# One kernel, two decoder layers: two heads' scores with one zero-padded key tile, and matmuls of different column tiles issued in turn

## The chip, the cores and the metric

The kernel runs on one core of a Trainium2 chip. The metric is the device time of one execution, in microseconds (us), lower is better. The core has a matmul engine (TensorE, "PE" in profile rows, with its weight loads as "PEld"), three element-wise engines (VectorE "DVE", ScalarE "ACT", GpSimd "POOL") and a queue that issues transfers (SyncE, "SP"). Each engine works through its own instructions in order and waits for others by semaphores.

## The reference, cut to what matters

Two layers are computed for a prompt of 512 tokens and for 8 samples of 4 tokens each (32 sample tokens). Layer 0 has 8 attention heads of width 64 beside a convolution branch; layer 1 is a gated linear recurrence. The change touches the attention of layer 0 alone. For the prompt it is causal attention over all 512 positions (two blocks of 256, both always chosen):

```python
s_own = jnp.einsum('bhqd,bhkd->bhqk', qc, k_own).astype(jnp.float32) * scale
...
p = jax.nn.softmax(s, axis=-1)
...
return (jnp.einsum('bhqnk,bhqnkd->bhqd', p_sel, v_sel)
        + jnp.einsum('bhqk,bhkd->bhqd', p_own, v_own))
```

For each sample the queries meet 256 cached positions (two pages of 128, found by a page table) and the sample's own 4 new positions.

## The kernel before, in words

All activations lie transposed, features on the 128 partitions and tokens along the free axis. A projection is a sum of `unit` calls (L136 to L145): one unit is 24 matmuls of 128x128 weights with 272 columns, on a high and a low part of weights and inputs (L142, L143, L144). Weight tiles arrive by `wtile`, which also splits them on ScalarE (`wh`, L133) and VectorE (`wl`, L134).

The attention of the prompt works on one pair of heads at a time, `c` = 0 to 3. The 64 features of the pair's first head lie on partitions 0 to 63, those of the second on 64 to 127. `prep(c)` projects q, k, v and the gate, normalises them and transposes the keys into `kT` (L430, one ScalarE copy of 128x512). `attend(...)` then goes over four query blocks `i` of 128 rows. For each head `hh` it computes the scores (L465, 64 rows of contraction, 128, 256, 384 or 512 columns), adds a causal mask with a bfloat16 matmul (L467), takes the maximum (L473, VectorE), the exponential (L476, ScalarE), divides (L478), transposes 128x128 pieces of the probabilities through TensorE (L102), copies them back (`PT`, L483, ScalarE) and multiplies with the values (L485, an output of 64 partitions at `tile_position` 0 or 64). The score tiles `s` have two PSUM banks, the transposes `t` two, the output `o` one.

A matmul of 32-bit operands is two matmul instructions on the engine, each with its weight load; the 64 score products are 32 in the code, the 160 value products 80 and the 128 key products of the samples 64. Transposes are one each.

The samples' stage (L569 to L611) loads each sample's two cached key pages (`kn`, 256 KB each, 8 buffers, by SP) and multiplies them with block-diagonal queries `qbd`: 4 chunks `c` for each page (L576, an output of 32 partitions at `tile_position` 32*n4), for samples n4 = 0 to 3 of a group `g`, with both pages `j` of one sample before the next sample. The new keys follow (L582), then a softmax over 288 columns, then the value pages (`kn` again, L611). The 8 `kn` buffers are shared with squares, sums and the conv gate of layer 0, so pages wait for buffers.

A scheduler decides the order on every engine from the code's order and priorities; `attend` runs at a raised priority, and `unit` work of other stages is put between its steps. Beside all this VectorE does the convolution, 120 multiply-adds of 128x512 (L508). The functions that the diff touches:

Of the kernel before, what the change touches and what calls it, by code (L numbers as in the profile page):

```python
# [9 lines left out]
F32 = mybir.dt.float32  # L10
# [3 lines left out]
AF = mybir.ActivationFunctionType  # L14
# [5 lines left out]
TP = 512  # L20
# [46 lines left out]
def hybrid_step(ctx, tc, xt_in, cache_kt, cache_v, conv_in, hgrn_in, page_table, par_in, k_norm_0,  # L67
# [3 lines left out]
    V, A, G, PE, SP = nc.vector, nc.scalar, nc.gpsimd, nc.tensor, nc.sync  # L71
# [7 lines left out]
    def nm(s):  # L79
        cnt[0] += 1  # L80
        return f"{s}{cnt[0]}"

    def mk(pool, tag, shape, bufs, dt=F32):
        return pool.tile(shape, dt, name=nm(tag), tag=tag, bufs=bufs)

    def bank(tag, cols=512, dt=F32):
        return pp.tile([128, cols], dt, name=nm(tag), tag=tag, bufs={"g": 3, "s": 2, "t": 2, "o": 1}[tag])
# [13 lines left out]
    def transpose(out, in_, np_):  # L101
        PE.transpose(out, in_, ident[:np_, :np_])  # L102

    def split(hi, lo, src, eng=None):
        A.activation(hi, src, AF.Copy)
        (eng or V).tensor_tensor(lo, src, hi, op=ALU.subtract)
# [44 lines left out]
    gq8 = cp.tile([128, 1], F32, name="gq8")  # L151
# [22 lines left out]
    def mtile(key, dt=F32R):  # L174
        m_[key] = mk(hp, "m", [128, T], 2 * KT, dt)
        return m_[key]

    with tc.tile_pool(name="l0", bufs=1) as lp:
# [138 lines left out]
        qbd = lp.tile([128, 4, NS, 32], F32, name="qbd")  # L317
# [51 lines left out]
            uconv(c)  # L369

        aes = ExitStack()

        def prep(c):
            col = c * 128
# [8 lines left out]
            pk = bank("t")  # L383
# [11 lines left out]
            qT = mk(lp, "qT", [128, T], 2)  # L395
# [16 lines left out]
            for hh in range(2):  # L412
                r = slice(64 * hh, 64 * hh + 64)
# [1 line left out]
                V.scalar_tensor_tensor(qbd[r, c, :, o:o + 4], qT[r, TP:T].rearrange("p (n t) -> p n t", t=4),  # L415
                                       gq8[r], rq[r, 8:40].rearrange("p (n t) -> p n t", t=4),
                                       op0=ALU.mult, op1=ALU.mult)
            kT = mk(lp, "kT", [128, TP], 2)
            for i0, i1, n in ((0, 4, 128), (4, 5, TS)):
                k3 = kt[:n, i0:i1].rearrange("p i (h d) -> p (i h) d", d=64)  # L420
                nb = 2 * (i1 - i0)
# [4 lines left out]
            pk = bank("t")  # L426
            pks = bank("t")
            for i, n, sl in TOK:
                transpose(pk[:, sl] if i < 4 else pks[:, :n], kt[:n, i], n)
            A.activation(kT, pk, AF.Copy, scale=gq8[:, 0:1])  # L430
            V.tensor_copy(ksT[:, c], pks[:, :TS])

            w = wtile(w_in_0, 1024 + col)
# [4 lines left out]
            pk = bank("t")  # L438
# [19 lines left out]
        def attend(c, rq, qT, kT, vt, ga):  # L458
            po = bank("o")
            for i in range(4):  # L460
                L = 128 * (i + 1)
                ss = [bank("s"), bank("s")]
                for hh in range(2):
                    r = slice(64 * hh, 64 * hh + 64)
                    PE.matmul(ss[hh][:, :L], qT[r, i * 128:(i + 1) * 128], kT[r, 0:L], start=True, stop=False)  # L465
                for hh in range(2):
                    PE.matmul(ss[hh][:, L - 128:L], identb, causb, start=False, stop=True)  # L467
                for hh in range(2):
                    r = slice(64 * hh, 64 * hh + 64)
                    rqc = rq[:, 2 * i + hh:2 * i + hh + 1]  # L470
                    s = ss[hh]
                    mx = mk(lp, "mx", [128, 4], 4)
                    V.tensor_reduce(mx[:, 0:1], s[:, :L], axis=AX.X, op=ALU.max, negate=True)  # L473
                    A.activation(mx[:, 1:2], mx[:, 0:1], AF.Copy, scale=rqc)
                    P = mk(qp, "PP", [128, 512], 3)
                    A.activation(P[:, :L], s[:, :L], AF.Exp, bias=mx[:, 1:2], scale=rqc, accum_out=mx[:, 2:3])  # L476
                    V.reciprocal(mx[:, 3:4], mx[:, 2:3])
                    V.tensor_scalar_mul(P[:, :L], P[:, :L], mx[:, 3:4])  # L478
                    pT = bank("t")
                    for j in range(i + 1):  # L480
                        transpose(pT[:, j * 128:(j + 1) * 128], P[:, j * 128:(j + 1) * 128], 128)
                    PT = mk(qp, "PT", [128, 512], 3)
                    A.activation(PT[:, :L], pT[:, :L], AF.Copy)  # L483
                    for j in range(i + 1):
                        PE.matmul(po[r, i * 128:(i + 1) * 128], vt[:, j, r],  # L485
                                  PT[:, j * 128:(j + 1) * 128], start=(j == 0), stop=(j == i),
                                  tile_position=(0, 64 * hh))
            mh, ml = mtile(("h", c)), mtile(("l", c))
            V.scalar_tensor_tensor(ga[:, :TP], po, 0.5, ga[:, :TP], op0=ALU.mult, op1=ALU.mult)
            split(mh[:, :TP], ml[:, :TP], ga[:, :TP])  # L490
# [9 lines left out]
        qp = aes.enter_context(tc.tile_pool(name="qk", bufs=1))  # L500

        p0 = prep(0)
        p1 = prep(1)
        with tc.high_priority(offset=300):
            attend(*p0)
        for c in (0, 1, 2, 3):
            for j in range(1, 31):
                V.scalar_tensor_tensor(cy[c][:, :TP], up[c][:, j:j + TP], cw[:, c, j:j + 1], cy[c][:, :TP],  # L508
                                       op0=ALU.mult, op1=ALU.add)

        p2 = prep(2)
        with tc.high_priority(offset=300):
            attend(*p1)
# [24 lines left out]
        with tc.high_priority(offset=300):  # L538
            attend(*p2)
# [25 lines left out]
        ss_, PTs = [], []  # L565
        for g in range(2):
            s = bank("s", 288)
            ss_.append(s)
            for n4 in range(4):  # L569
                n = 4 * g + n4  # L570
                for j in range(2):
                    knT = mk(lp, "kn", [128, T], 8)[:, :512]
                    rg = SP.value_load(pt[0:1, 2 * n + j:2 * n + j + 1], min_val=0, max_val=cache_kt.shape[0] - 1)
                    SP.dma_start(knT, cache_kt[bass.ds(rg, 1)].rearrange("a p c t -> (a p) (c t)"))
                    for c in range(4):
                        PE.matmul(s[32 * n4:32 * n4 + 32, j * 128:(j + 1) * 128], qbd[:, c, n, :],  # L576
                                  knT[:, c * 128:(c + 1) * 128], start=(c == 0), stop=(c == 3),
                                  tile_position=(0, 32 * n4))
            PE.matmul(s[:, 256:288], identb, smb[:, 32 * g:32 * g + 32], start=True, stop=False)
            for n4 in range(4):  # L580
                for c in range(4):
                    PE.matmul(s[32 * n4:32 * n4 + 32, 256:288], qbd[:, c, 4 * g + n4, :], ksT[:, c, :],  # L582
                              start=False, stop=(c == 3), tile_position=(0, 32 * n4))
        for g in range(2):
            s = ss_[g]
# [10 lines left out]
            PT = mk(qp, "PT", [128, 512], 3)  # L596
# [4 lines left out]
        for g in range(2):  # L601
            PT = PTs[g]
            ov = bank("s")
            PE.matmul(ov, PT[:32, 256:384], vsn, start=True, stop=False)
            for j in range(2):
                for n4 in range(4):
                    n = 4 * g + n4
# [4 lines left out]
                              start=False, stop=(j == 1), tile_position=(0, 32 * n4))  # L612
# [406 lines left out]
```

## Time and profile before

| | us |
|---|---|
| three runs | 694.25, 694.40, 694.69 (median 694.4) |
| the profiled execution | 693.45 |
| its span in the trace | 691.7 |
| TensorE busy | 671.8 |
| VectorE busy | 542.6 |
| ScalarE busy | 314.5 |
| GpSimd busy | 70.3 |
| mean granted TensorE clock | 0.99 |

The span runs from the first to the last instruction that the profiler recorded; the profiled execution's own time has 1.75 us around it. "Busy" is the time in which at least one instruction of the engine was running; matmuls overlap in a pipeline, so a TensorE that is busy all the time can still do less per microsecond than it could.

### The profile page before, as it was taken

How to read it: one execution, taken by the hardware profiler on the slowest of the kernel's cores; microseconds unless marked ns; L12 is line 12 of the kernel's file. 1: busy time of each engine (PE TensorE's matmuls, PEld its weight loads, DVE VectorE, ACT ScalarE, POOL GpSimd, SP SyncE). 2: the span in 40 equal slices, each digit the busy share in tenths (PEclk: the TensorE clock that was granted, in tenths of full speed). 3: DMA queues.
4: the chain of work that ended last, by engine and by line, in shares of the span. 5: the costliest groups of instructions: out<-in, count | busy, mean ns of one | idle time of the engine just before them, and what ended most of it. 6: DMA issues, size and time to landing. Idle time of an engine off the chain costs nothing.

```text
span 691.7 us, 14812 instructions
## 1 busy us (share of the span) xinstructions
PE 671.8 (97%) x5806; PEld 598.3 (86%) x5806; DVE 542.6 (78%) x1326; ACT 314.5 (45%) x758; POOL 70.3 (10%) x89
## 2 busy tenths in 40 slices
PE   8899999989999999999998999999999999999997
PEld 7799999867877976857998999989998989899997
DVE  7999999898957975344796987878697878777676
ACT  7332444525556956232665453525253525234221
POOL 5000200000302100000001200102020202020100
PEclk9999999989999999999999999999999999999999
DMA  9412152221111150674454213141313131322213
GB/s 268 155 62 92 65 167 79 77 77 32 56 69 30 63 170 1 176 234 132 159 177 150 65 62 125 64 127 62 127 62 128 62 127 62 111 63 68 76 52 142
DMA packets 34583, 70.51 MB, mean 102 GB/s; under 512 B 7378, under 2 KB 16210, under 8 KB 34514
## 3 DMA queue, kind: packets, MB, share of 16 engines
q1 hardware_dynamic: 34514, 69.58, 31.3%
q8 instruction: 45, 0.74, 0.4%
q14 instruction: 24, 0.20, 0.1%
HBM read 59.84 MB, written 9.73 MB: 101 GB/s over the span
## 4 chain that ended last, share of the span: by engine, by line
PE 91%; DVE 5%; ACT 1%; issue 1%; DMA 1%; SPq 1%; DVEq 0%
PE g L142 22%; PE g L144 22%; PE g L143 22%; PE t L102 5%; PE s L465 3%; PE o L485 3%; PE s L576 2%; PE s L611 2%; PE s L768 1%; PE t L874 1%; PE o L887 1%; PE o L889 1%; DVE wl L134 1%; PE t L907 1%; DMA wr<-in_w_in_dram 1%
## 5 line engine op out<-in xcount | busy, mean ns | idle before, releaser
L142 PE MATMUL g<-h,wh 128*128 128x272 f32 x944 | 277.8, 295 | 7.1 <-ACT f L702 2.6
L143 PE MATMUL g<-h,wh 128*128 128x272 f32 x944 | 276.1, 293 | 2.1 <-DVE h L273 2.1
L144 PE MATMUL g<-h,wl 128*128 128x272 f32 x944 | 276.5, 293 | 0.0
L142 PEld LDWEIGHTS g<-h,wh 128*128 128x128 f32 x944 | 179.7, 191 | 11.5 <-ACT f L702 3.1
L143 PEld LDWEIGHTS g<-h,wh 128*128 128x128 f32 x944 | 179.7, 191 | 4.0 <-DVE h L273 2.8
L144 PEld LDWEIGHTS g<-h,wl 128*128 128x128 f32 x944 | 179.7, 191 | 2.0 <-issue 1.3
L133 ACT ACTIVATE wh<-wr 128x1024 fp32r<-128x1024 f32 (+4 forms) x90 | 88.2, 982 | 109.4 <-PE g L143 101.9
L134 DVE TENSOR_TENSOR wl<-wr,wh 128x1024 fp32r<-128x1024 f32 (+4 forms) x90 | 101.1, 1125 | 22.8 <-ACT wh L133 22.6
L508 DVE SCALAR_TENSOR_TENSOR m<-m,vecs,m 128x512 f32<-128x512 f32 x120 | 84.1, 734 | 0.0
L143 PE MATMUL g<-m,wh 128*128 128x272 f32 x256 | 74.4, 293 | 0.0
L144 PE MATMUL g<-m,wl 128*128 128x272 f32 x256 | 73.5, 290 | 0.0
L142 PE MATMUL g<-m,wh 128*128 128x272 f32 x256 | 73.1, 295 | 0.0
L143 PEld LDWEIGHTS g<-m,wh 128*128 128x128 f32 x256 | 48.2, 188 | 4.3 <-issue 3.1
L142 PEld LDWEIGHTS g<-m,wh 128*128 128x128 f32 x256 | 47.1, 188 | 4.5 <-issue 2.1
L144 PEld LDWEIGHTS g<-m,wl 128*128 128x128 f32 x256 | 48.1, 188 | 1.2 <-DVE tb L642 0.8
L473 DVE TENSOR_REDUCE mx<-s 128x1 f32<-128x128 f32 (+3 forms) x32 | 15.4, 485 | 13.3 <-PE s L467 13.1
L483 ACT ACTIVATE PT<-t 128x128 f32<-128x128 f32 (+3 forms) x32 | 13.9, 434 | 26.0 <-PE t L102 25.7
L485 PE MATMUL o<-PT,vt 128*64 128x128 f32 x160 | 23.9, 283 | 1.6 <-ACT PT L483 1.5
L465 PE MATMUL s<-kT,qT 64*128 64x128 f32 (+3 forms) x64 | 25.2, 482 | 0.0
L910 DVE SCALAR_TENSOR_TENSOR S<-S,tot,t 128x128 f32<-128x128 f32 x64 | 17.7, 342 | 6.3 <-PE t L907 6.2
L485 PEld LDWEIGHTS o<-PT,vt 128*64 128x64 f32 x160 | 16.4, 136 | 6.0 <-ACT PT L483 2.5
L852 DVE TENSOR_TENSOR kk<-kk,tot 128x256 f32<-128x256 f32 (+1 forms) x48 | 20.0, 417 | 0.0
(289 smaller groups left out, 998.6 us busy)
## 6 DMA issues: line engine op xcount, KB each, us to landing
wr<-in_w_in_dram SPq DMA_DIRECT2D x58, 512.0 KB, 3.6
wr<-in_w_out_dram SPq DMA_DIRECT2D x16, 512.0 KB, 3.6
kn<-in_cache_kt_dram SPq DMA_DIRECT2D x16, 256.0 KB, 2.9
kn<-in_cache_v_dram SPq DMA_DIRECT2D x16, 256.0 KB, 3.3
S<-in_hgrn_dram SPq DMA_DIRECT2D x8, 512.0 KB, 3.7
out_hgrns_dram<-S SPq DMA_DIRECT2D x8, 512.0 KB, 2.6
xTall<-in_xt_dram SPq DMA_DIRECT2D x8, 272.0 KB, 4.9
out_y_dram<-xTall SPq DMA_DIRECT2D x8, 272.0 KB, 2.4
```

The lines of the kernel that those rows point to most:

```text
L102: PE.transpose(out, in_, ident[:np_, :np_])
L133: A.activation(wh, raw, AF.Copy)
L134: V.tensor_tensor(wl, raw, wh, op=ALU.subtract)
L142: PE.matmul(ps, wh[:, k - k0, :], ah, start=(k == k0), stop=False)
L143: PE.matmul(ps, wh[:, k - k0, :], al, start=False, stop=False)
L144: PE.matmul(ps, wl[:, k - k0, :], ah, start=False, stop=(k == k1 - 1))
L465: PE.matmul(ss[hh][:, :L], qT[r, i * 128:(i + 1) * 128], kT[r, 0:L], start=True, stop=False)
L473: V.tensor_reduce(mx[:, 0:1], s[:, :L], axis=AX.X, op=ALU.max, negate=True)
L485: PE.matmul(po[r, i * 128:(i + 1) * 128], vt[:, j, r], PT[:, j * 128:(j + 1) * 128], start=(j == 0), stop=(j == i), tile_position=(0, 64 * ...
L508: V.scalar_tensor_tensor(cy[c][:, :TP], up[c][:, j:j + TP], cw[:, c, j:j + 1], cy[c][:, :TP], op0=ALU.mult, op1=ALU.add)
L852: V.tensor_tensor(k3[:, :, 0, :], k3[:, :, 0, :], t3[:, :, 1:2].to_broadcast([128, nblk, hsz]), op=ALU.mult)
L910: V.scalar_tensor_tensor(S0[:, n, :], S0[:, n, :], tots[:, n:n + 1], pn[:, n4 * 128:(n4 + 1) * 128], op0=ALU.mult, op1=ALU.add)
```

## The change

The keys of a pair go into a tile `kz` of 128 x 2 x 512, which has zeros where the other head's features would be; GpSimd clears it once, and ScalarE fills it with two copies of 64x512 in place of one of 128x512. A score product then contracts over all 128 partitions with the same 128x128 weight `qT` for both heads. The value products of a block are written after both heads' softmax, alternating between the heads. The samples' key products take the four samples of a group in turn for each chunk, all with their first pages and then all with their second pages, and so do the products with the new keys.

```diff
+        kz = [lp.tile([128, 2, TP], F32, name=f"kz{b}") for b in range(2)]
+        for b in range(2):
+            for hh in range(2):
+                G.memset(kz[b][64 - 64 * hh:128 - 64 * hh, hh], 0.0)
...
-            kT = mk(lp, "kT", [128, TP], 2)
+            kT = kz[c % 2]
...
-            A.activation(kT, pk, AF.Copy, scale=gq8[:, 0:1])
+            for hh in range(2):
+                r = slice(64 * hh, 64 * hh + 64)
+                A.activation(kT[r, hh], pk[r], AF.Copy, scale=gq8[r, 0:1])
...
                 for hh in range(2):
-                    r = slice(64 * hh, 64 * hh + 64)
-                    PE.matmul(ss[hh][:, :L], qT[r, i * 128:(i + 1) * 128], kT[r, 0:L], start=True, stop=False)
+                    PE.matmul(ss[hh][:, :L], qT[:, i * 128:(i + 1) * 128], kT[:, hh, 0:L], start=True, stop=False)
...
-                    for j in range(i + 1):
+                    PTs.append(PT)
+                for j in range(i + 1):
+                    for hh in range(2):
+                        r = slice(64 * hh, 64 * hh + 64)
                         PE.matmul(po[r, i * 128:(i + 1) * 128], vt[:, j, r],
-                                  PT[:, j * 128:(j + 1) * 128], start=(j == 0), stop=(j == i),
+                                  PTs[hh][:, j * 128:(j + 1) * 128], start=(j == 0), stop=(j == i),
                                   tile_position=(0, 64 * hh))
...
-            for n4 in range(4):
-                n = 4 * g + n4
-                for j in range(2):
+            for j in range(2):
+                kns = []
+                for n4 in range(4):
+                    n = 4 * g + n4
                     knT = mk(lp, "kn", [128, T], 8)[:, :512]
...
-                    for c in range(4):
-                        PE.matmul(s[32 * n4:32 * n4 + 32, j * 128:(j + 1) * 128], qbd[:, c, n, :],
-                                  knT[:, c * 128:(c + 1) * 128], start=(c == 0), stop=(c == 3),
+                    kns.append(knT)
+                for c in range(4):
+                    for n4 in range(4):
+                        PE.matmul(s[32 * n4:32 * n4 + 32, j * 128:(j + 1) * 128], qbd[:, c, 4 * g + n4, :],
+                                  kns[n4][:, c * 128:(c + 1) * 128], start=(c == 0), stop=(c == 3),
                                   tile_position=(0, 32 * n4))
...
-            for n4 in range(4):
-                for c in range(4):
+            for c in range(4):
+                for n4 in range(4):
                     PE.matmul(s[32 * n4:32 * n4 + 32, 256:288], qbd[:, c, 4 * g + n4, :], ksT[:, c, :],
```

The scheduler keeps the order on VectorE the same up to the end of the first pair's attention, and on SP throughout. On TensorE it moves what the code moves. Two places show it; a row gives line, operation, output and inputs by name, the output's shape and a count.

On TensorE, in the attention of the third pair (query blocks 1 and 2, `PT` are the transposed probabilities of one head each), before:

```order
L102 MATMUL t_2506<-cst,PP_2502 128x128 x2
L485 MATMUL o_2448<-PT_2495,vt_1861 64x128 x2
L102 MATMUL t_2526<-cst,PP_2522 128x128 x3
L465 MATMUL s_2552<-kT_1786,qT_1714 128x512
L467 LDWEIGHTS identb
L467 MATMUL s_2552<-causb,identb 128x128
L485 MATMUL o_2448<-PT_2509,vt_1861 64x128 x2
L102 MATMUL t_2542<-cst,PP_2538 128x128 x3
```

and with the change:

```order
L102 MATMUL t_2510<-cst,PP_2506 128x128 x2
L493 MATMUL o_2454<-PT_2501,vt_1867 64x128
L102 MATMUL t_2532<-cst,PP_2528 128x128 x3
L470 MATMUL s_2558<-kz_735,qT_1720 128x512
L472 LDWEIGHTS identb
L472 MATMUL s_2558<-causb,identb 128x128
L493 MATMUL o_2454<-PT_2513,vt_1867 64x128
L493 MATMUL o_2454<-PT_2501,vt_1867 64x128
L493 MATMUL o_2454<-PT_2513,vt_1867 64x128
L102 MATMUL t_2545<-cst,PP_2541 128x128 x3
```

The two value products of one head stood together, a step apart from those of the other head. Now the first product of the first head stands alone where its `PT` is ready, and the other products of both heads follow together, after the second head's `PT`.

On TensorE, where the samples' key products begin, between the last value products of the fourth pair (`kn` with a number is one page), before:

```order
L576 MATMUL s_3080<-kn_3081,qbd 32x128 x4
L576 MATMUL s_3080<-kn_3096,qbd 32x128 x4
L576 MATMUL s_3080<-kn_3111,qbd 32x128 x4
L576 MATMUL s_3080<-kn_3126,qbd 32x128
L485 MATMUL o_2598<-PT_2696,vt_2370 64x128 x3
L102 MATMUL t_2714<-cst,PP_2710 128x128 x4
L576 MATMUL s_3080<-kn_3126,qbd 32x128 x3
L576 MATMUL s_3080<-kn_3141,qbd 32x128 x4
L102 MATMUL t_2732<-cst,PP_2728 128x128 x4
L576 MATMUL s_3080<-kn_3156,qbd 32x128 x4
```

and with the change, from the last chunk of the first group of four pages:

```order
L587 MATMUL s_3086<-kn_3109,qbd 32x128
L587 MATMUL s_3086<-kn_3120,qbd 32x128
L587 MATMUL s_3086<-kn_3147,qbd 32x128
L493 MATMUL o_2604<-PT_2699,vt_2376 64x128
L493 MATMUL o_2604<-PT_2686,vt_2376 64x128
L493 MATMUL o_2604<-PT_2699,vt_2376 64x128
L493 MATMUL o_2604<-PT_2686,vt_2376 64x128
L493 MATMUL o_2604<-PT_2699,vt_2376 64x128
L102 MATMUL t_2720<-cst,PP_2716 128x128 x4
L102 MATMUL t_2734<-cst,PP_2730 128x128 x4
L587 MATMUL s_3086<-kn_3158,qbd 32x128
L493 MATMUL o_2604<-PT_2725,vt_2376 64x128
```

One page's four products stood together, page after page. Now the first four pages' 16 products stand together, chunk by chunk (the last two are the first two rows), followed by one product of the fifth page (`kn_3147`), and the first product of the sixth (`kn_3158`) comes after 5 value products and 8 transposes. A page's buffer is free again only when the last chunk of its group is done.

## Rows read from the trace of the kernel before

**Rows 1.** The page: the chain that ended last, its shares by engine.

```profile
PE 91%; DVE 5%; ACT 1%; issue 1%; DMA 1%; SPq 1%; DVEq 0%
```

**Rows 2.** By stage: start:end, length, busy PE, PEld, DVE, ACT, POOL, clock, DMA share, GB/s.

```profile
100.00:165.00 65.00, 61.59 (x424) 53.89 (x424) 60.35 (x114) 28.06 (x61) 0.66 (x1) 0.95 0.25 75
...
250.00:285.00 35.00, 34.68 (x220) 22.58 (x221) 15.12 (x44) 18.91 (x54) 0.00 (x0) 1.00 0.29 89
285.00:325.00 40.00, 40.00 (x289) 25.42 (x287) 19.67 (x42) 14.00 (x32) 0.00 (x0) 1.00 0.55 178
```

**Rows 3.** Timeline of TensorE around 170 us (start, length, instructions, idle before).

```profile
168.67 1.09 PE L485 MATMUL o<-PT,vt 128*64 128x128 f32 x8 [0.69 <-ACT PT L483]
169.69 0.70 PE L465 MATMUL s<-kT,qT 64*128 64x256 f32 x2
...
170.38 0.60 PE L102 MATMUL t<-cst,PP 128*128 128x128 f32 x4
170.82 0.60 PE L102 MATMUL t<-cst,kr 128*128 128x128 f32 x4
```

**Rows 4.** The same view around 271 us, scores of 512 columns.

```profile
270.45 1.12 PE L465 MATMUL s<-kT,qT 64*128 64x512 f32 x2
271.51 0.23 PE L467 MATMUL s<-causb,identb 128*128 128x128 bf16 x1
271.57 0.50 PE L102 MATMUL t<-cst,PP 128*128 128x128 f32 x3
272.00 1.12 PE L465 MATMUL s<-kT,qT 64*128 64x512 f32 x2
```

**Rows 5.** The chain of waits (start, length, what): scores of 128 columns, first pair.

```profile
107.11 0.42 PE s L465 x4
...
164.39 0.42 PE s L465 x2
```

**Rows 6.** The chain of waits, samples' stage.

```profile
284.92 0.99 PE s L576 x8
...
299.14 0.83 PE s L582 x32
```

**Rows 7.** The chain of waits, layer 1: products on four column tiles in turn.

```profile
418.94 0.57 PE t L897 x16
```

**Rows 8.** Timeline of TensorE, value pages of the samples.

```profile
300.95 1.06 PE L611 MATMUL s<-kn,PT 128*32 128x512 f32 x6
302.51 1.05 PE L611 MATMUL s<-kn,PT 128*32 128x512 f32 x2
```

**Rows 9.** Timeline of TensorE in layer 1: one product alone on one column tile.

```profile
454.47 0.41 PE L901 MATMUL s<-c,cst 128*32 128x128 f32 x2
454.81 0.73 PE L907 MATMUL t<-ve,kts 128*128 128x512 f32 x2
```

**Rows 10.** The chain of waits around 135 us.

```profile
132.70 2.51 DVE m L508 x4
...
137.15 2.65 DVE m L508 x4
```

**Rows 11.** The stage behind that wait, columns as in rows 2.

```profile
140.00:147.00 7.00, 6.51 (x28) 5.99 (x29) 7.00 (x12) 1.55 (x5) 0.00 (x0) 0.52 0.15 45
```

**Rows 12.** Timeline of SP: issues of key pages (start, from first issue to last).

```profile
246.69 1.55 SPq L574 DMA_DIRECT2D kn<-in_cache_kt_dram  x3
...
276.17 0.35 SPq L574 DMA_DIRECT2D kn<-in_cache_kt_dram  x1
```

**Rows 13.** The tile `kn`: time of its transfers.

```profile
DMA to landing us min/median/max: 2.5/2.9/5.4
```

**Rows 14.** The line of the `kT` copy (duration in ns, min/median/max).

```profile
L430 ACT ACTIVATE kT<-t,gq x4: 667/678/688, 103.1 to 247.7; 128x512 f32<-128x512 f32 x4
```

**Rows 15.** Timeline of GpSimd at the start.

```profile
0.88 0.95 POOL L318 MEMSET qbd<- 128x1024 f32 x1
...
4.12 1.09 POOL L186 TENSOR_TENSOR kn<-xTall 128x544 f32<-128x544 f32 x1 [2.29 <-DMA xTall<-in_xt_dram]
```

More of the change, by code (lines that the diff above doesn't have):

```diff
@@ L463, in attend @@
                 for hh in range(2):
-                    r = slice(64 * hh, 64 * hh + 64)
-                    PE.matmul(ss[hh][:, :L], qT[r, i * 128:(i + 1) * 128], kT[r, 0:L], start=True, stop=False)
+                    PE.matmul(ss[hh][:, :L], qT[:, i * 128:(i + 1) * 128], kT[:, hh, 0:L], start=True, stop=False)
                 for hh in range(2):
                     PE.matmul(ss[hh][:, L - 128:L], identb, causb, start=False, stop=True)
+                PTs = []
                 for hh in range(2):
-                    r = slice(64 * hh, 64 * hh + 64)
                     rqc = rq[:, 2 * i + hh:2 * i + hh + 1]
```

## The prediction, made before the changed kernel was run

> **What bounds the kernel now.** I read the chain of waits first, since it says what the end waited for: TensorE holds 91% of it [rows 1]. Then the stages: all that differs lies between 100 and 325 us, and in the last 75 of these TensorE is busy almost without a gap while VectorE and ScalarE are busy for half the time or less [rows 2]. Before 165 us it is otherwise: VectorE works 60.35 of 65 us. So a microsecond taken off TensorE is worth a microsecond in the later stages, less in the first. The question is how much of TensorE's busy time is work; the timeline, read from the start of one group to the start of the next, answers that.
>
> **Scores.** Two instructions of 128 columns (one product) take 0.42 us, two of 512 columns 1.06 us until the mask begins [rows 5, 4]. The difference, 0.64 us for twice 384 columns, is 0.107 us per 128 columns, so 0.21 us of each block of scores doesn't depend on its size. Another 0.10 lies ahead of it: three transposes before the second block take 0.43 us [rows 4], where four before other transposes take 0.44 [rows 3], 0.11 each. I read this 0.31 us as the price of a change from the full array to a tile of it, with the weight load uncovered, and back. With zero padding the scores use the full array, as transposes, masks and projections do. The built program has 31 blocks of scores before (9.6 us of such price) and 32 after, of which 9 follow value products and still pay 0.20 (1.8); the other 23 pay nothing by [rows 3], where transposes follow transposes without a gap, and at most 0.10 each, the lowest price seen at a change; I take 0.02 (0.5). The columns that stream stay the same. One thing is lost: where both heads stood together, four instructions took the 0.42 us of two [rows 5]; that was one pair of 16, 0.2 us. Drains at 7 changes from values to scores before and 9 after are counted under both, which adds 0.2 to the gain. Scores: 9.6 - 1.8 - 0.5 - 0.2 + 0.2 = 7.3 us less.
>
> Here a page speaks against the change. The Trainium skill (TensorE: Matmul & The Clock Gate, section "Why this matters for your kernels") says that products with few contraction rows should be put on distinct row groups, where they run at the same time, and padding gives that up. The trace agrees for the one pair that stood together [rows 5]; by the rule alone the padded scores would be dearer by that 0.2 us for every pair issued together.
>
> **Values.** Eight instructions take 1.02 us until the next group starts [rows 3]: 8 x 0.11 and 0.14; with 0.10 on entry a block costs 0.24 beside its products. Products on different column tiles share the time: 16 instructions on four tiles in turn take 0.57 us [rows 7], 4 x 0.11 and 0.13, and value pages on three tiles take no longer than on one [rows 8]. So two heads in turn should cost as much as one. But the scheduler issues the first head's first product alone. Before: 80 products x 0.22, less 0.2 where two heads stood together, and 31 x 0.24 = 24.8 us. After, with blocks of 1, 3, 5 and 7 products in the main (29 of them), I count 54 rounds x 0.22 + 29 x 0.24 = 18.9. Gain 5.9.
>
> **Samples.** A page's eight instructions take 0.99 us [rows 6], 0.11 beyond 8 x 0.11, 0.21 with entry: 64 x 0.22 + 11 blocks x 0.21 = 16.4 us. After, four tiles in turn: 22 rounds x 0.22 + 9 x 0.23 = 6.9. Gain 9.5. The new keys, 32 instructions in 0.83 us [rows 6], are 0.026 each and so overlap little now; four tiles in turn would take 8 x 0.026 + 0.13. Gain between nothing and 1.0 for both groups, I take 0.5. The value products' code is as it was, but one block fewer results from the new order: 0.97 us by [rows 8] if pages arrive in time, nothing otherwise; I take 1.0.
>
> Sum of TensorE's savings: 7.3 + 5.9 + 9.5 + 0.5 + 1.0 = 24.2 us.
>
> **What is given back.** (1) At 133 us TensorE waits for VectorE, which runs convolution steps, the keys' scaling, and more convolution [rows 10]. VectorE's order there is unchanged, so what TensorE gains ahead of it (three full blocks of scores, 0.7 us) is spent waiting. Behind it the clock is at 0.52, near the lower level of 1.2 GHz [rows 11], after TensorE had idled; I count no change of that. (2) From 140 to 285 us some 12 us are saved, 7 of them in 250 to 285, where 28 us would remain for 18.9 us of ScalarE and 15.1 of VectorE [rows 2]. No engine becomes the bound, but each head is a chain from scores over maximum, exponential and transposes back, with two score banks. I take 2.0 lost; between 0 and 6, which is half. (3) Key pages. Pages 6 to 8 take the buffers of pages 1 to 3, now free only when the group's 16 products are done. An issue follows the other by some 0.6 us [rows 12], landing takes 2.9 [rows 13]: page 6 is there 3.1 us and page 8 4.3 us after the first group. In the meantime TensorE has 5 value products (3 rounds, 0.9) and 8 transposes (1.0): it waits 1.2 us, and behind that wait stand the fourth pair's last value products and the projections of the output. The third group has 2.4 us of cover for 3.1 (0.7 waited), the fourth about 2.2 (0.9). Together 2.8, I take 3.0. From below 1, as the first five pages were in early and only the sixth waited for a buffer, at 276.17 [rows 12]; from above three whole groups of 4.6 us, 13.8. (4) Two copies of 64x512 in place of one: a copy takes 0.68 us [rows 14] and I take each half to take as long, since the columns stay 512: 2.7 us of ScalarE, of which one copy is waited for, 0.7 (0 to 2.7). (5) Four memsets of 512 columns are 4 x 0.5 us by the one of 1024 (0.95) and fit in GpSimd's 2.29 us of waiting for its input [rows 15]: 0; without that cover 2.0.
>
> Sum: 24.2 - 0.7 - 2.0 - 3.0 - 0.7 = 17.8 us. The profiled execution took 693.45, so 675.65; the median of the runs lies 0.95 above it: **676.6**, 2.6% faster.
>
> **The rivals.** *All of it arrives*: pages come in time, the chains of the heads have slack, and 22 to 25 us go: 670 to 672. For: the stages of 250 to 325 us. Against: the buffers. *Half is given back*: the heads' chains and the pages take 6 and 7, and one more stall brings the lower clock for 7 us as in [rows 11], 3.4 us of work: 24 - 17 = 7, so 687. For: TensorE's idle piece of 0.69 us at [rows 3], where the cover of the probabilities' copy is already gone. *No overlap*: products in turn don't share the time, and each change of tile costs as a lone product does, 0.34 us [rows 9] where 0.22 streams. Then the samples' 64 products cost 22 us (5 more), the 80 value products 29 (4 more), and with the scores' 7 less the kernel takes about 697, slower. Against: [rows 7, 8]. *Page waits make it slower*: each of three groups waits its full 4.6 us, and each wait lowers the clock (3.4 us of work): 24 us, which is where it decides; beyond it, with the value pages late too, some 697. Against: five pages are there at the start and the cover worked out above. *It doesn't do what it says*: no sign; the built order shows the new sequences.
>
> **How the numbers follow.** My forecast (12 to 21 us less, 673 to 682) gets 0.60, all of it 0.15, half given back 0.17, no overlap 0.04, page waits 0.03, a result within 0.2% 0.01. The range 668 to 687 leaves out the two slower cases, and the far ends; the likeliest alone has 673 to 682. A measurement of this kernel can tell about 0.2% (1.4 us) from no change: faster 0.91, same 0.03, slower 0.06, with some weight moved from half given back to the last two, as its lower end is open.
>
> **What would show it.** In the profile after: blocks of scores of 512 columns at 0.86 us to the mask's start where transposes precede; a block of seven value products in about 1.1 us; the first 16 key products in about 1 us; waits of TensorE for pages of 1 us or more between the groups; TensorE's busy time near 650. I am wrong if value products in turn start 0.11 us or more apart throughout, if the samples' stage keeps its length, or if the lower clock turns up around the key pages.

## The result, and the profile after

The changed kernel takes 674.8 us in the median of its runs (673.57 to 677.64), the kernel before 694.3: the ratio is 0.9725 with an interval of 0.9692 to 0.9759, 2.4% to 3.1% faster. The forecast was 676.6 in a range of 668 to 687. The profiled execution is the fastest of the four; its span is 670.7 us, 21.0 less than before.

The page of the changed kernel has TensorE's busy time and the chain that ended last by engine, to be read beside [rows 1].

```profile
PE 646.7 (96%) x5806; PEld 583.2 (87%) x5806; DVE 541.8 (81%) x1326; ACT 313.8 (47%) x760; POOL 70.1 (10%) x93
...
PE 88%; DVE 6%; DMA 2%; ACT 2%; issue 1%; SPq 1%; DVEq 0%
```

TensorE is busy 25.1 us less (671.8 before) and idle 4.1 us more (24.0 in place of 19.9): 25.1 less 4.1 is the span's 21.0. The number of TensorE's instructions is the same, 5806, so what changed is how closely they follow each other and, for 3.4 us of the span, at which clock. The chain of work that ended last now holds 2% of transfers, where it held 1%.

By stage, columns as in [rows 2] and [rows 11]:

```profile
100.00:165.00 65.00, 60.33 (x440) 54.31 (x439) 61.42 (x118) 30.73 (x67) 0.22 (x1) 0.97 0.25 78
140.00:147.00 7.00, 6.78 (x36) 5.64 (x37) 7.00 (x13) 2.87 (x8) 0.00 (x0) 0.77 0.15 42
250.00:285.00 35.00, 33.63 (x373) 22.31 (x373) 20.74 (x57) 20.74 (x60) 0.00 (x0) 1.00 0.40 126
285.00:325.00 40.00, 40.00 (x269) 31.45 (x269) 24.76 (x41) 19.21 (x34) 0.00 (x0) 1.00 0.59 193
```

In the 35 us from 250 TensorE does 373 matmul instructions where it did 220. VectorE's share from 100 to 165 us has risen to 61.42 of 65. Behind the wait near 136 us the clock is at 0.77 over seven microseconds, where it was 0.52: the stretch at the lower level (1.2 GHz) lasts 3.4 us in place of 6.8.

TensorE's timeline at the places that the prediction named (start, length, instructions, idle before):

```profile
254.27 1.09 PE L493 MATMUL o<-PT,vt 128*64 128x128 f32 x14
255.29 0.70 PE L470 MATMUL s<-kz,qT 128*128 128x256 f32 x2
...
260.25 1.02 PE L470 MATMUL s<-kz,qT 128*128 128x512 f32 x2
261.11 0.22 PE L472 MATMUL s<-causb,identb 128*128 128x128 bf16 x1
...
263.93 1.28 PE L587 MATMUL s<-kn,qbd 128*32 128x128 f32 x34
265.14 0.87 PE L493 MATMUL o<-PT,vt 128*64 128x128 f32 x10
...
267.61 0.41 PE L587 MATMUL s<-kn,qbd 128*32 128x128 f32 x2 [0.58 <-DMA kn<-in_cache_kt_dram]
...
269.59 1.06 PE L587 MATMUL s<-kn,qbd 128*32 128x128 f32 x26 [0.21 <-DMA kn<-in_cache_kt_dram]
...
270.70 0.46 PE L593 MATMUL s<-ksT,qbd 128*32 128x32 f32 x32
...
279.53 0.41 PE L587 MATMUL s<-kn,qbd 128*32 128x128 f32 x2 [0.58 <-DMA kn<-in_cache_kt_dram]
```

A padded product of 512 columns reaches its mask after 0.86 us, where it took 1.06 [rows 4]. Seven value products (14 instructions, two column tiles in turn) leave TensorE free after 1.02 us, which is what four took before [rows 3]. Seventeen key products take 1.21 us, where four took 0.99 [rows 6]; the new keys' 32 instructions take 0.46 in place of 0.83 [rows 6]. The three waits for key pages (the DMA releases in brackets) are what the change costs in return; the prediction looked for waits of 1 us or more there, and none is longer than 0.58.

To put the 25.1 us on the parts I took the time from each instruction's start to the next one's, over the whole of both traces, and counted it for the first of the two; what a step takes beyond its usual spacing is kept apart, as waiting or, in the stretches at the lower level, as the clock's.

| us from start to start | before | after |
|---|---|---|
| scores | 23.1 | 17.3 |
| transposes and projections (what stands ahead of a tile) | 487.6 | 485.2 |
| value products | 21.7 | 15.9 |
| key products of pages | 14.3 | 6.6 |
| new keys | 1.5 | 0.5 |
| value pages | 10.8 | 9.8 |
| all of TensorE's work | 624.0 | 599.9 |
| lost in stretches at the lower clock | 7.2 | 5.1 |
| waiting, 100 to 165 us | 4.7 | 7.4 |
| waiting, 165 to 250 us | 10.0 | 10.9 |
| waiting, 250 to 330 us | 3.1 | 4.8 |
| waiting, elsewhere | 37.5 | 37.4 |

The other instructions, 65.0 and 64.6 us of the work, have no row. Work is 24.1 less, waiting 5.2 more, the loss at the lower clock 2.1 less: 21.0. How much counts as waiting depends on what is called usual. With the median of all steps between the same two kinds of instruction, work comes out 22 to 23 us less and the clock's loss 3.5 less; the rows of the changed parts hold within 1 us.

### The profile page after: what moved, and what is told of

It reads as the page before. It is cut to its first block, busy times and chain, and to the rows that moved or that the text cites. A ratio compares the mean times of both kernels' runs of the same rounds, so it can differ in the third digit from the quotient of the medians.

```text
span 670.7 us, 14828 instructions
## 1 busy us (share of the span) xinstructions
PE 646.7 (96%) x5806; PEld 583.2 (87%) x5806; DVE 541.8 (81%) x1326; ACT 313.8 (47%) x760; POOL 70.1 (10%) x93
## 4 chain that ended last, share of the span: by engine, by line
PE 88%; DVE 6%; DMA 2%; ACT 2%; issue 1%; SPq 1%; DVEq 0%
PE g L142 23%; PE g L144 22%; PE g L143 22%; PE t L102 4%; PE s L470 3%; DVE m L516 2%; PE o L493 2%; PE s L622 1%; PE s L779 1%; PE t L885 1%; DVE wl L134 1%; PE o L898 1%; PE o L900 1%; DMA kn<-in_cache_kt_dram 1%; DMA wr<-in_w_in_dram 1%
## 5 line engine op out<-in xcount | busy, mean ns | idle before, releaser
L470 PE MATMUL s<-kz,qT 128*128 128x128 f32 (+3 forms) x64 | 23.7, 454 | 1.2 <-ACT PP L481 1.2
L481 ACT ACTIVATE PP<-s,mx,rq 128x128 f32<-128x128 f32 (+3 forms) x32 | 19.7, 616 | 0.5
L914 POOL TENSOR_TENSOR ve<-vx,cst 128x1024 fp32r<-128x1024 f32 x8 | 15.9, 1985 | 37.5 <-PE t L918 17.7
```

Source lines behind the costliest of these rows:

```text
L470: PE.matmul(ss[hh][:, :L], qT[:, i * 128:(i + 1) * 128], kT[:, hh, 0:L], start=True, stop=False)
L914: G.tensor_tensor(ve, vx.unsqueeze(1).to_broadcast([128, NS, 128]), exm.unsqueeze(2).to_broadcast([128, NS, 128]), op=ALU.mult)
```

## The experiments

**One part alone.** Three kernels had one part of the diff each.

> The kernel before with the padded scores alone (the cleared tile, the two copies of the keys, 128 rows of contraction). If the price lies in the change to a tile and back, a block of scores loses 0.29 us where a transpose or a projection stands ahead (24 of 32 in the built order) and 0.1 where a value product does (8), 7.8 us, less 0.2 for the pair that stood together; with 0.7 lost at VectorE's wall, 0.7 for the second copy and about 1 in the heads' chains: 687.5 to 690 us. If the number of contraction rows were what counts (products of 64 rows share the time when they stand together), padding gains nothing: 694 to 695.

> The kernel before with the alternating value products alone. If products on two column tiles share the time: 5.9 us less on TensorE, about 1 us of it lost in the heads' chains, 688 to 690 us. If they don't share it and each change of tile costs 0.11 us more, about 698. If only the heads' chains counted, no change, 694.

> The kernel before with the samples' key products and new keys in turn alone. If four tiles in turn share the time: 8.6 us less for the pages, 1.0 for the new keys, 1 to 2 for value pages (9 blocks in place of 11), and 1.5 to 3 given back by waits for pages whose buffers come free only with the whole group: 684.5 to 687 us. If the page waits eat the gain: 691 or more, with waits of several us on TensorE for kn.

| | median | ratio, interval | TensorE busy |
|---|---|---|---|
| padded scores | 686.6 | 0.9898 (0.9875 to 0.9921) | 661.2 |
| alternating values | 683.7 | 0.9851 (0.9825 to 0.9878) | 658.0 |
| samples' keys | 686.0 | 0.9887 (0.9860 to 0.9914) | 658.7 |

Each is faster by itself, so three rivals fall: that padding gains nothing, that products on different column tiles don't overlap, and that page waits eat the gain. Padding came out 7.2 us faster, a little more than expected, the keys 7.9, as expected. The values gave 10.1 where 4 to 6 were expected. Their own products fell from 21.7 to 15.8 us, as in the whole; but the scheduler, finding TensorE earlier, also built 9 blocks of key products and 9 of value pages where there were 11 of each (1.3 and 1.9 us). Its profile also loses 3.2 us at the lower clock in place of 7.2, but that belongs to these two executions: over the runs the mean granted clock is 0.991 and that of the kernel before 0.993. A part's gain is thus not its own products alone: whatever comes earlier is merged differently.

**Two parts together.** The changed kernel without the padding:

> The changed kernel with the scores as before (64 rows, one copy of the keys), that is, values and samples' keys together. The three parts alone gave 7.2, 10.1 and 7.9 us, 25.2 in sum, the whole 19.5. If the missing 5.7 us are blocks of key products and value pages that two parts both merged (11 to 9 blocks of each in the run of the values alone, 11 to 10 and 9 in that of the keys) and a lower-clock stretch near 140 us that each part alone shortened: padding is still worth its 6 to 7 us in company, and this kernel takes 680.5 to 682.5. If instead padding loses its worth once the others are there (the chains take it): 676 to 678.

It took 679.3 us, ratio 0.9792 (0.9777 to 0.9807). Values and keys give 14.4 together, not 18.0: their merged blocks are partly the same. Key products are at 6.6 and value pages at 9.8 as in the whole, where the sum of both parts' savings would be 1.3 and 1.7 lower. Padding is worth 0.67% of the time before in this company, 4.6 us, uncertain by 2.6; that lies between both expectations. The traces show why it isn't more. From this kernel to the changed one TensorE's work falls by 7.8 us, counted as in the table above, and waiting rises by 3.6 between 100 and 250 us, where VectorE has few gaps and the softmax chains run. The runs of the changed kernel also lose 2.0 us more to the lower clock (see the clock's part, below).

**Lone value products.** The built order left the first head's first product alone, and I had counted 0.46 us for each such step. The edit of the next run, and of one that spares the first pair:

```diff
                 for j in range(i + 1):
-                    for hh in range(2):
+                    for hh in (1, 0):
```

```diff
                 for j in range(i + 1):
-                    for hh in range(2):
+                    for hh in ((0, 1) if c == 0 else (1, 0)):
```

> The changed kernel with the second head's value product written ahead of the first head's in each turn, so that no product of the first head is issued alone: 16 blocks of value products in place of 29 and 40 rounds in place of 54. If a lone product costs its round (0.22 us) and its change of tile (0.24): about 6 us less on TensorE, 668.5 to 671 us. If the lone product stood where TensorE waited for the softmax anyway, the time goes to that wait: 673 to 675.

> The changed kernel with the second head's value product first in the second to fourth pairs alone; the first pair, whose attention stands beside the convolution on VectorE, stays as in the changed kernel. The built order has 20 blocks of value products in place of 29. If the earlier run with all four pairs lost its gain to the wall behind VectorE at 174 us and the lower clock after it: about 4 us less on TensorE, and 670.5 to 672 us. If the lone products stood in waits for the softmax in the later pairs too: 674 to 676.

All four pairs: 674.7 us, ratio 0.9718 (0.9693 to 0.9744), no gain over the changed kernel. Pairs two to four alone: 670.7 us, ratio 0.9661 (0.9642 to 0.9680), 4 us faster (uncertain by 2.7), the best of all here. In the first, value products fell from 15.9 to 11.3 us, and all of it went elsewhere. TensorE's timeline after the first pair's last values, with all four pairs reversed:

```profile
173.78 0.29 PE L144 MATMUL g<-h,wl 128*128 128x272 f32 x1
176.89 0.39 PE L142 MATMUL g<-h,wh 128*128 128x272 f32 x1 [2.82 <-ACT ga L247]
```

and its stages from 172 and from 212 us:

```profile
172.00:182.00 10.00, 7.18 (x45) 6.96 (x44) 9.95 (x23) 4.97 (x9) 0.00 (x0) 0.83 0.11 27
212.00:222.00 10.00, 7.49 (x48) 6.45 (x44) 9.52 (x17) 6.26 (x12) 3.27 (x5) 0.83 0.02 5
```

In the changed kernel the same wait is 1.31 us, and the clock in both stretches 1.00. So TensorE comes there 0.7 us earlier, goes on 0.8 later, while VectorE works 9.95 of 10 us, and then runs 3.4 us at the lower level. It does so once more behind a wait of 2.51 us near 215 us; there the changed kernel waits as long (2.53) and keeps its clock, so this second stretch can't be laid to the order of the products. The kernel that spares the first pair keeps the 1.31 us there, and its clock:

```profile
172.00:182.00 10.00, 8.69 (x69) 8.47 (x69) 9.84 (x23) 5.34 (x11) 0.14 (x1) 1.00 0.18 54
```

In the later pairs a lone product costs about what I counted: 9 blocks fewer take 2.8 us off the value products, and by the 0.09 of an entry some 0.8 ahead of them (an estimate), 3.6 where 4.1 were counted. But the span of the profile falls by 2.4 us only, with 2.0 more of idle time and 5 less at the lower clock, so the 4 us of the medians are in part the clock's (below). In the first pair the time saved went to the wait at 174 us; that a lone product there fills a wait is the likely reading, not a shown one.

**Waits for key pages.** Two runs. The first lets every group read the first group's pages:

```diff
                     kns.append(knT)
+                kn4 = kn4 or kns
...
-                                  kns[n4][:, c * 128:(c + 1) * 128], start=(c == 0), stop=(c == 3),
+                                  kn4[n4][:, c * 128:(c + 1) * 128], start=(c == 0), stop=(c == 3),
```

> The changed kernel, but every group's key products read the first group's four pages; all 16 key pages are still loaded. It leaves out the use of key pages 5 to 16. So no product waits for a page and all 16 of a group stand together (4 blocks of 20, 12, 15 and 17 in place of 9). If the waits and lone products cost what the trace of the changed kernel shows (2.1 us of waits at three places and five blocks of 0.24 more): 3 us faster, 671 to 672.5. If the projections put between the groups hide them: within 0.2%, 674 to 676.

It took 678.4 us, ratio 0.9770 (0.9749 to 0.9791), 3.6 us slower than the changed kernel (uncertain by 2.8). Its key products were over at 271.9 us, 9.5 earlier, and then TensorE waited for a value page:

```profile
280.20 1.91 PE L624 MATMUL s<-kn,PT 128*32 128x512 f32 x2 [4.69 <-DMA kn<-in_cache_v_dram]
```

with 6.8 us at the lower clock behind it. As a price of the key pages' waits this run says nothing: the four tiles that it reads all along are four buffers fewer for the value pages, which is the likely reason why these come late. The other run has ten buffers; the room for them comes from leaving the padding out, so it is compared with a kernel of the next pair that differs by the buffers alone (696.6 us, 1.0039, 1.0023 to 1.0054).

```diff
-                    knT = mk(lp, "kn", [128, T], 8)[:, :512]
+                    knT = mk(lp, "kn", [128, T], 10)[:, :512]
```

(and so at the other four places of `kn`.)

> The first kernel of this call with ten buffers for pages in place of eight (the cleared tile's room allows it there): 6 blocks of key products in place of 9 and 8 of value pages in place of 10. If waits for key pages cost what they seem to in the changed kernel (2.1 us at three places, 0.24 for a block): 2.5 to 4 us less than the first. If the transfers themselves bound the pages (the wait goes to the value pages, as where the key products read only the first four): within 1 us of the first, with waits at value pages.

693.3 us, ratio 0.9986 (0.9971 to 1.0002): 3.3 us less than its partner, in the range of the first theory. The mean granted clock of both kernels' runs is 0.971, so the clock has no part in it. Its waits for key pages, and after them those of the partner:

```profile
288.41 1.06 PE L588 MATMUL s<-kn,qbd 128*32 128x128 f32 x26 [1.25 <-DMA kn<-in_cache_kt_dram]
...
292.99 1.07 PE L588 MATMUL s<-kn,qbd 128*32 128x128 f32 x28 [1.02 <-DMA kn<-in_cache_kt_dram]
```

```profile
290.57 0.41 PE L588 MATMUL s<-kn,qbd 128*32 128x128 f32 x2 [1.28 <-DMA kn<-in_cache_kt_dram]
...
292.92 1.06 PE L588 MATMUL s<-kn,qbd 128*32 128x128 f32 x26 [0.58 <-DMA kn<-in_cache_kt_dram]
...
304.55 1.06 PE L588 MATMUL s<-kn,qbd 128*32 128x128 f32 x26 [1.18 <-DMA kn<-in_cache_kt_dram]
```

With the small ones (0.22 in the first; 0.15 and 0.16 in the second) the waits are 2.5 us beside 3.4. Most of the gain lies in the blocks that stand whole: key products without these waits take 6.6 us from start to start in place of 7.5, value pages 7.9 in place of 9.8.

**Rows or tiles.** Does padding win because a change of tile costs, or would 64-row products side by side do better? Two pairs of kernels held both heads' scores together, padded and in halves. In the first pair the products and masks were one unit for the scheduler:

```diff
-                for hh in range(2):
-                    PE.matmul(ss[hh][:, :L], qT[:, i * 128:(i + 1) * 128], kT[:, hh, 0:L], start=True, stop=False)
+                with tc.tile_critical():
+                    for hh in range(2):
+                        PE.matmul(ss[hh][:, :L], qT[:, i * 128:(i + 1) * 128], kT[:, hh, 0:L], start=True, stop=False)
...
```

> The changed kernel with both heads' padded scores and both masks of a query block held together on TensorE (16 blocks of two products in place of 32 of one). It is the partner of the next run, from which it differs by the padding alone. Products of 128 rows follow each other at their full length, so a block of two times 512 columns should take 1.72 us to its first mask. The first head's softmax begins later by the second head's product: 674.5 (the gain of fewer blocks behind value products covers it) to 679 us.

> As the run above, but with 64 rows for each head, as in the kernel before (no cleared tile, one copy of the keys), the heads' products next to each other. If products on the two halves of the rows share the time, two times 512 columns take 1.06 us to the mask, a block costs 0.29 us for entry and exit, and all scores 13.2 us of TensorE in place of about 17.7: 4 to 5 us faster than the run above, and if the chains allow it faster than the changed kernel too. If they don't share it, every block pays 0.29 us more than the padded one: 4 to 5 us slower than the run above.

722.5 us (1.0398, 1.0380 to 1.0416) and 716.2 (1.0320, 1.0296 to 1.0345). The halves are 6.3 us faster, a little more than expected, but both are far slower than forecast: the unit waits for other engines, and VectorE waits for its end. TensorE's idle time between instructions is some 47 us in both profiles, from 19 in the changed kernel, and the time at the lower clock 61 and 75 us, from 12. VectorE's timeline in the second:

```profile
154.60 1.02 DVE L474 TENSOR_REDUCE mx<-s 128x1 f32<-128x384 f32 x2 [2.04 <-PEq L463]
```

So I tried it with the two score banks as one tile, on the 670.7 us kernel:

```diff
-                ss = [bank("s"), bank("s")]
+                s2 = sp[0].tile([128, 2, 512], F32, name=nm("s"), tag="s2")
+                ss = [s2[:, 0], s2[:, 1]]
...
```

> The faster kernel of the earlier runs (second head's value product first in pairs two to four, 670.7 us) with 64 rows for each head again and both heads' score banks taken as one tile of two banks, so that the heads' products stand next to each other (15 of 16 pairs in the built order) without a hold on the other engines. The earlier two runs with joined heads had 17.3 us of TensorE in padded scores and 8.9 in halves. If that carries over: 7 us less on TensorE than in the padded partner of this call (8.4 less 16 entries at 0.09 more), minus what the chains lose because a block's scores wait for both heads' exponentials: 662 to 669 us, and 5 to 8 below the partner. If the chains (VectorE up to 175 us, two score banks) are what bounds this stretch, both stand within 2 us of each other.

> The partner: the same with padded scores (128 rows), so it differs from the 670.7 us kernel only by the heads' scores standing together (14 of 16 pairs) and waiting for both banks. TensorE's work as there within 1 us; if the chains have slack, 670 to 672; if each of 16 blocks loses the 0.3 to 0.7 us by which the second head's exponential ends after the first's, 674 to 680.

Halves 696.6 us, padded 697.0 (1.0049, 1.0028 to 1.0070). One block of two times 512 columns, in halves:

```profile
280.52 1.13 PE L469 MATMUL s<-kT,qT 64*128 64x512 f32 x4 [0.19 <-ACT PP L480]
281.59 0.28 PE L471 MATMUL s<-causb,identb 128*128 128x128 bf16 x2
```

and padded:

```profile
256.19 1.98 PE L474 MATMUL s<-kz,qT 128*128 128x512 f32 x4 [0.19 <-ACT PP L485]
258.01 0.27 PE L476 MATMUL s<-causb,identb 128*128 128x128 bf16 x2
```

1.07 us beside 1.82: products on the two halves of the rows do share the time. The Trainium skill (TensorE: Matmul & The Clock Gate, section "Why this matters for your kernels") says that products in distinct row groups run at the same time; the trace agrees. The scores of the halves take 7 us less of TensorE in all, as expected, and still both kernels stand within half a microsecond, 26 above the kernel they were made from. A block's scores now wait for both exponentials of the block before. The halves' timeline shows what takes the time:

```profile
262.19 0.88 PE L492 MATMUL o<-PT,vt 128*64 128x128 f32 x12 [0.58 <-ACT PT L487]
264.54 0.63 PE L103 MATMUL t<-cst,PP 128*128 128x128 f32 x4 [1.48 <-DVE PP L482]
...
268.19 1.12 PE L492 MATMUL o<-PT,vt 128*64 128x128 f32 x8 [0.93 <-ACT PT L487]
```

TensorE waits at one step of the softmax after the other; its idle time between instructions is 39.5 us in both, from 21.2 in the 670.7 us kernel. The other part of the loss is the clock. From 165 and from 250 us, halves first and padded second:

```profile
165.00:250.00 85.00, 76.23 (x558) 66.87 (x559) 61.80 (x141) 50.79 (x111) 5.67 (x8) 0.94 0.21 61
250.00:290.00 40.00, 28.19 (x201) 16.95 (x199) 17.60 (x48) 20.40 (x58) 0.00 (x0) 0.83 0.18 61
```

```profile
165.00:250.00 85.00, 75.89 (x589) 68.01 (x588) 63.91 (x149) 53.94 (x117) 5.10 (x8) 1.00 0.24 75
250.00:290.00 40.00, 27.59 (x195) 16.69 (x197) 14.12 (x41) 19.09 (x54) 0.00 (x0) 0.91 0.13 40
```

The halves stand at the lower level for 37 us of the span, the padded scores for 20, the 670.7 us kernel for 7. The 17 us between the first two are up to 8.5 us of work at half the clock, about what the shared rows gain. My expectation that the chains lose 0.3 to 0.7 us a block was too low: 18.3 us more of idle time over 16 blocks are 1.1 each, and I hadn't counted that the idle time brings the lower clock.

**The clock's part.** Every run lists its span and mean granted clock. At the lower level the granted share is one half, so (1 - mean clock) x span is the most that a run lost by it. Means over the runs of each kernel, in us:

| | span | lost by the clock, at most | the rest |
|---|---|---|---|
| the changed kernel | 672.9 | 6.9 | 666.0 |
| without the padding | 677.5 | 4.9 | 672.6 |
| second head first, all pairs | 672.5 | 7.8 | 664.7 |
| second head first, pairs two to four | 668.7 | 4.3 | 664.4 |
| score banks joined, halves | 694.6 | 20.4 | 674.2 |
| score banks joined, padded | 695.1 | 14.0 | 681.1 |

So up to 2.6 of the 4 us between the changed kernel and the fastest one are the clock's, and up to 3.5 of the 3.8 between the two reversed orders. By the last column padding is worth 6.6 us in company, and the joined halves stand 6.9 us below the joined padded scores.

## Why the prediction was right

**Scores: 7.3 predicted.** Scores themselves 5.8 less and most of the 2.4 from what stands ahead of them; 7.8 in the step from the kernel without padding. The price of 0.31 for a change of tile and back came out at 0.29: entry 0.20 falls to 0.11 behind a transpose, the step inside the product and the exit by 0.10 each. Behind a value product only the exit is saved, as taken. The Trainium skill (TensorEngine Tiling (Array Packing), section "Key Properties") says that a change of tiling mode drains the engine, without a price. The trace fits it with the 0.10 at the exit, but doesn't show a drain as such.

**Values: 5.9 predicted, 5.8 measured** (21.7 to 15.9). That two column tiles share the time held everywhere; the loss to lone products was in the built order and was counted.

**Samples: 9.5 predicted, 7.7 measured** from start to start, some 0.2 more with the entries of two blocks fewer. This term was too big: I priced 64 products at 0.22, but in the kernel before the products of one sample's last chunk and the next sample's first already shared time inside a block (26 instructions there start within 2.35 us, where 25 steps of 0.109 would be 2.7). That is 1.0 us of it; the blocks after took 0.6 more than counted. **New keys: 0.5 taken, 1.0 measured**, its upper bound. **Value pages: 1.0 and 1.0.**

The sum, 24.2, meets the 24.1 measured partly by luck: samples 1.8 too big, new keys 0.5 and scores up to 0.9 too small.

**Given back: 6.4 predicted, 5.2 measured in waits, less 2.1 that the clock gave.** Here the forecast was least right: 3.1 net where 6.4 were taken. The wall at 133 us (0.7) did not work as I said. TensorE came to the keys' transposes 0.9 us earlier and left them as much earlier, so VectorE, whose order is the same, was not the fixed end that I took it for. In the kernel before and after, its waits there are:

```profile
137.37 0.65 PE L102 MATMUL t<-cst,kr 128*128 128x128 f32 x4 [0.61 <-ACT kT L430]
139.96 0.40 PE L102 MATMUL t<-cst,kr 128*32 128x128 f32 x1 [1.94 <-DVE ksT L431]
```

```profile
137.14 0.66 PE L102 MATMUL t<-cst,kr 128*128 128x128 f32 x4 [1.29 <-ACT kz L436]
139.05 0.28 PE L102 MATMUL t<-cst,kr 128*32 128x128 f32 x1 [1.25 <-DVE ksT L437]
```

The second copy is there (0.61 becomes 1.29, one copy of 0.68), and it disappears in the wait for VectorE behind it (1.94 becomes 1.25): the 0.7 that I counted for the copies cost nothing here. What I had at no change, the clock behind this wait, gave most of the 2.1 us in this pair of profiles. It isn't a gain of the change: the runs of the changed kernel have a mean clock of 0.990, those of the kernel before beside the single parts 0.993. Why its lower stretch is 3.4 us there and not 6.8 isn't settled: the kernel with values and keys alone has the 6.8, and so has the 670.7 us kernel.

In their place 2.7 us of waiting came in the whole stretch from 100 to 165 us, where VectorE is full; the chains from 165 to 250 cost 0.9 of the 2.0; the pages, 3.0 predicted, cost 1.7 in the stage. Their three waits add up to 1.4 us where 2.8 were worked out, and none reaches the 1 us that was named as a sign. Ten buffers gained 3.3 us in another kernel, but only 0.9 of that were waits. Four memsets took their 2.2 us beside other work, as counted.

**The rivals.** "All of it arrives" would have needed 670 to 672 us; the four runs took 673.6 to 677.6, median 674.8, inside the likeliest case. "Half is given back" didn't happen, but its mechanism is real: with all pairs reversed, more waiting and two more stretches at the lower clock took all that the value products saved, and scores that wait for both heads cost 26 us. "No overlap" and "page waits make it slower" fell with the single parts.

## What to carry to other kernels

Where TensorE is the bound, look at spacing before work: the 5806 instructions stayed 5806, and some 24 us went from changes of tile (0.29 us for a block of scores) and from products on different column tiles that stood one behind the other. Work saved on TensorE counts only where it doesn't wait for another engine: the same edit was worth 4 us in three pairs and nothing when the first, beside a full VectorE, was included, so try such an edit stage by stage. Compare the granted clock of all runs before you explain 2 us: here up to 2.6 of those 4 were the clock's. And a faster pairing of instructions is no gain if it makes two chains wait for each other: count what the waiting instruction needs before counting what it saves.

## What the runs showed of the hardware

The lower clock doesn't follow the length of a wait alone: after an idle piece of 2.53 us at 213 us the changed kernel kept the clock at 1.00, after one of 2.51 at 215 us the kernel with all values reversed had 3.4 us at the lower level. A 32-bit product on the full array behind a product on a column tile still pays inside itself: 0.21 us lie between the two instructions of a 128-column score behind value products, 0.11 behind a transpose. And two products on different column tiles start within 0.01 us of each other, so 17 on four tiles need 1.21 us: five rounds of 0.22, and 0.1 to leave the tiles.
